# A decoder layer's start: the order of the first loads, who squares x, and where two projections stand

## The chip, the cores and the metric

The kernel runs on one core of one Trainium2 chip. The core has five engines that run side by side, each through its own list of instructions in order: PE (matrix products and transposes, into PSUM), DVE and POOL (elementwise work; POOL does not reach PSUM), ACT (elementwise functions, copies, scaling) and SP, which here only issues transfers (DMA). ACT can issue transfers too. The metric is the device time of one execution in microseconds; lower is better. One run of the kernel before was also profiled.

## The reference, cut to what matters

One layer, 512 tokens, width 1024, float32. It normalises x, makes one wide projection, and sends its columns through a state-space branch and an attention branch.

```python
h = rms_norm(x, norm_w[layer])
proj = h @ w_in[layer]
u_s, z_s, q, k, v, z_a, r_s, r_a = jnp.split(proj, offsets, axis=-1)
y_s = s5_branch(u_s, lam_re, lam_im, log_dt, b_re, b_im, c_re, c_im, d_skip, w_glu)
y_s = (y_s * jax.nn.silu(z_s)) @ w_ssm_out
q, k = rope(rms_norm(q, ...)), rope(rms_norm(k, ...))
y_a = (dilated_attention(q, k, v) * jax.nn.silu(z_a)) @ w_attn_out
m = jax.nn.sigmoid(r_s) * y_s + jax.nn.sigmoid(r_a) * y_a
x = x + m @ w_o
```

`s5_branch` is a linear recurrence over time with a complex diagonal A of 64 groups x 64 states, made from `lam_re`, `lam_im` and `log_dt`; B (`b_re`, `b_im`: 64 x 64 x 16 each) feeds it, C reads it. `dilated_attention` takes three groups of heads and joins them by their softmax sums.

## The kernel before, in words

**Precision and projections.** Each float32 operand of a large product is split into a rounded high part and a low rest, and `mm3` (L107) adds three products: high-high, high-low, low-high. A weight tile (128 rows x 8 x 128 columns, 512 KB) is loaded by `load_w` (L162) into `w_raw`, of which there are two buffers; ACT writes `w_hi` (L93), and DVE or POOL writes `w_lo` (L95); of these pairs there are three. `plan` (L112 to L149) lists all weight tiles in order, `get_w` takes the next one and calls for the loads two tiles ahead. A projection of 128 columns for all 512 tokens (`cm_unit`, L172) is 24 matmuls.

**The start.** SP loads x in four pieces of 512 KB (L193), with the first two weight tiles between them; for those two the low part is written by POOL (`lo_w`, L191). Tokens are taken in two halves. For each, ACT squares and sums two pieces (L208), DVE makes the reciprocal root in eleven small steps (L99, L210), ACT and DVE scale x (L214, L216), PE transposes it (L223), and ACT and DVE write the two parts of the transposed, normalised `hT` (L227, L228). The first three projections run on the first half of the tokens and then on the second (L287 to L292).

**The state-space tables.** `lam_re`, `lam_im` and `log_dt` are loaded by SP (L298 to L300), and some hundred small DVE operations make the powers of A from them (L303 to L378); PE transposes these into `AT` and `fT` (L388, L394). B is loaded into tile `dd` (L408): `D1` holds real over imaginary part, `D2` imaginary over real part, 64 partitions each, so each half of B is loaded twice (L411 to L414). POOL negates one half of `D2` (L415), and DVE and POOL make `BB` and `BB2` (L422 to L427).

**W and X units, scan, Y.** For each of eight blocks of groups, `w_unit` (L263) forms coefficients (`coef`, DVE and POOL) and transposes them to W on PE; `x_unit` (L275) reads the projection u back through DRAM (`ud`) and multiplies it by W into `Xs`. When all eight are there, the scan runs on DVE (`scan_work`, L636, lines 590 to 634). Then the Y loop (L770) makes outputs block by block and `g_unit` applies GELU.

**Fillers.** `order` (L127) lists projections that depend on `hT` alone: gates `za`, `zs`, `rs`, values `v0`, `v`, and the first `n_ra` of eight `ra` units. `filler()` takes the next one. They stand between W and X units (L656), beside the scan (ten, L761) and in the Y loop (one per block, the rest after). The remaining `ra` units stand around the last head pair's softmax (L1019, L1022): while DVE and ACT do the softmax, PE does `ra` units up to `KT - 2`, then `values`, then the last two. In the W and X part, W0 follows the sixth `u` projection, W1 and X0 the seventh, W2, X1, W3 and X2 the eighth (L442 to L444).

**Who sets the order.** The program is written in one stream. When it is built, a planner plays it through with modelled durations and gives each engine its list: whatever is ready by the model goes when the engine is free, and earlier lines go first. On the chip this order is fixed, and each instruction waits for its real inputs. A transfer that waits stands in its issuing engine's list, and what is behind it waits too.

Of the kernel before, what the change touches and what calls it, by code (L numbers as in the profile page):

```python
# [11 lines left out]
F32 = mybir.dt.float32  # L12
F32R = mybir.dt.float32r
I32 = mybir.dt.int32
AF = mybir.ActivationFunctionType
ALU = mybir.AluOpType
# [4 lines left out]
P = 128  # L21
D = 1024
S = 512
KT = D // P
NB = S // P
G = 64
# [26 lines left out]
def tile_hybrid_block(ctx: ExitStack, tc: tile.TileContext, x, positions, norm_w, w_in, lam_re, lam_im,  # L53
# [19 lines left out]
    def scr(shape, dtype=F32):  # L73
        n = int(np.prod(shape[1:]))
        o = scr_o[0]
        scr_o[0] += n
        assert scr_o[0] <= 4096
        v = scr_t[0:shape[0], o:o + n]
        if len(shape) == 3:
            v = v.rearrange("p (a b) -> p a b", b=shape[2])  # L80
        elif len(shape) == 4:
            v = v.rearrange("p (a b c) -> p a b c", b=shape[2], c=shape[3])
        return v if dtype == F32 else v.bitcast(dtype)
# [26 lines left out]
        pe.matmul(o, ll, rh, start=False, stop=last, skip_group_check=True)  # L110

    plan, loaded, look = [], [], 2  # L112
    n_ra = 2
    lo_w = [dve]

    def section(w, k0, k1, *cols):
# [35 lines left out]
    def prefetch(n):  # L152
        while len(loaded) < min(n, len(plan)):
            loaded.append(load_w(*plan[len(loaded)]))
# [5 lines left out]
        return loaded[i]  # L160

    def load_w(srcs, kts, cols):  # L162
        raw = wp.tile([P, kts, cols], F32, name="w_raw", tag="w_raw", bufs=2)
        w = cols // len(srcs)
        for i, s in enumerate(srcs):
            sp.dma_start(raw[:, :, i * w:(i + 1) * w], s.rearrange("(k p) c -> p k c", p=P))
        hi = wp.tile([P, kts, cols], F32R, name="w_hi", tag="w_hi")
        lo = wp.tile([P, kts, cols], F32R, name="w_lo", tag="w_lo")
        split(hi, lo, raw, lo_eng=lo_w[0])
        return hi, lo  # L170
# [14 lines left out]
    nps = bank("nps")  # L185
    pe.transpose(nps[:, 0:KT], nw8, ident[:KT, :KT])
    dve.tensor_copy(nwc, nps[:, 0:KT])
    x_all = big.tile([P, NB, D], F32, name="x_all", tag="s3")
    x_t = [x_all[:, r] for r in range(NB)]
    xv = x[0].rearrange("(i r) d -> r i d", r=NB)  # L190
    lo_w[0] = pool  # L191
    for r in range(NB):
        sp.dma_start(x_t[r], xv[r])  # L193
        if r in (1, 2):
            prefetch(len(loaded) + 1)
    lo_w[0] = dve
    hT_hi = cst.tile([P, KT, S], F32R, name="hT_hi")
    hT_lo = cst.tile([P, KT, S], F32R, name="hT_lo")

# [2 lines left out]
    rst = scr([P, NB])  # L202
    ra_ = scr([P, NB])
    rb_ = scr([P, NB])
    junk = big.tile([P, D], F32, name="junk", tag="s6a")
    for h in range(2):
        for r in (2 * h, 2 * h + 1):
            act.activation(junk, x_t[r], AF.Square, accum_out=ss[:, r:r + 1])  # L208
        w = slice(2 * h, 2 * h + 2)
        dve.tensor_scalar(ms[:, w], ss[:, w], 1.0 / D, EPS, op0=ALU.mult, op1=ALU.add)  # L210
        rsqrt(rst[:, w], ms[:, w], [P, 2], ra_[:, w], rb_[:, w])
        for r in (2 * h, 2 * h + 1):
            if r % 2:
                act.activation(x_t[r], x_t[r], AF.Copy, scale=rst[:, r:r + 1])  # L214
            else:
                dve.tensor_scalar(x_t[r], x_t[r], rst[:, r:r + 1], None, op0=ALU.mult)  # L216
        for q in range(KT // 2):
            ps = bank("hps")
            pv = ps.rearrange("p (k r i) -> p k r i", k=2, r=2)
            for r in range(2):  # L220
                for k in range(2):
                    kk = 2 * q + k
                    pe.transpose(pv[:, k, r], x_t[2 * h + r][:, kk * P:(kk + 1) * P], ident)  # L223
            for k in range(2):
                kk, t = 2 * q + k, slice(256 * h, 256 * h + 256)
                src, w = ps[:, 256 * k:256 * k + 256], nwc[:, kk:kk + 1]
                act.activation(hT_hi[:, kk, t], src, AF.Copy, scale=w)  # L227
                dve.scalar_tensor_tensor(hT_lo[:, kk, t], src, w, hT_hi[:, kk, t].bitcast(F32),  # L228
                                         op0=ALU.mult, op1=ALU.subtract)
# [62 lines left out]
                mm3(ps[:, t], hi[:, k], lo[:, k], hT_hi[:, k, t], hT_lo[:, k, t], k == 0, k == KT - 1)  # L292
    for j in range(3):
        u_unit(j, first[j][1])
    lr = scr([G, N])
    li = scr([G, N])
    dt = scr([G, 1])
    sp.dma_start(lr, lam_re[0])  # L298
    sp.dma_start(li, lam_im[0])
    sp.dma_start(dt, log_dt.rearrange("o g -> g o"))  # L300


    def exp_exact(dst, src, shape, pfx):  # L303
# [101 lines left out]
        pool.tensor_scalar(A4[sl, 0, 1], ATv[sl, 1, h, :, 0], -1.0, None, op0=ALU.mult)  # L405


    dd = big.tile([P, 4, G, Q], F32, name="dd", tag="s1")  # L408
    D1, D2, BB, BB2 = (dd[:, i] for i in range(4))
    bv = [b_re[0].rearrange("g n q -> n g q"), b_im[0].rearrange("g n q -> n g q")]  # L410
    sp.dma_start(D1[0:64], bv[0])  # L411
    sp.dma_start(D1[64:128], bv[1])
    sp.dma_start(D2[0:64], bv[1])
    sp.dma_start(D2[64:128], bv[0])  # L414
    pool.tensor_scalar(D2[0:64], D2[0:64], -1.0, None, op0=ALU.mult)  # L415
    nca = 8 * 9 * Q
    abt = big.tile([P, 4096], F32, name="ab", tag="s5")
# [17 lines left out]
    def wx(*js):  # L435
        for j in js:
            if j < 8:
                Ws[j] = w_unit(j)
            if j > 0:
                x_unit(j - 1, Ws.pop(j - 1))  # L440

    for j in range(3, 8):  # L442
        u_unit(j)
        wx(*((), (), (0,), (1,), (2, 3))[j - 3])  # L444


    sza = cst.tile([P, NP, S], F32, name="sza")
# [205 lines left out]
        else:  # L653
            {"za": za_unit, "zs": zs_unit, "rs": rs_unit, "ra": ra_unit}[kind](c)

    for js in ((4,), (5, 6), (7, 8)):  # L656
        filler()
        wx(*js)

# [435 lines left out]
```

## Time and profile before

| what | value |
|---|---|
| device time, median of 3 runs | 743.52 us (743.5 to 743.62) |
| profiled execution, its own time | 745.33 us |
| its span, first to last instruction | 743.5 us |
| mean granted TensorE clock | 0.983 |
| PE matmul busy | 702.2 us (94%) |
| DVE busy | 468.4 us (63%) |
| ACT busy | 336.7 us (45%) |
| POOL busy | 168.7 us (23%) |
| data moved | 85.51 MB, mean 115 GB/s |

A line of the page reads: source line, engine, operation, output <- inputs, shapes, count; busy time and mean duration of one; idle time before, and who ended it. In the timeline a row begins with its start in us from the span's start and its duration; brackets at its end hold the idle time of the engine before it and what ended that. A "wait" row reads: who waited <- for whom: us in total, times, longest. `PEld` is PE's loading of weights, `SPq` and `ACTq` are the lists in which transfers are issued, so their duration is that of issuing, not of the transfer. The granted clock is 1.00 at full speed.

### The profile page before, as it was taken

Reading aid. Unit: us, or ns where it says so; the run is one execution under the profiler, and the core shown is the slowest. Engines: PE = TensorE matmul, PEld = TensorE weight load, DVE = VectorE, ACT = ScalarE, POOL = GpSimd, SP = SyncE. Lnnn points to the kernel's source line nnn. Section 1 sums busy time; section 2 is a strip of 40 time slices with the busy share of each in tenths; the row PEclk is TensorE's granted clock in tenths of the full one; section 3 lists DMA queues with packets and bytes.
Section 4 is the critical chain, followed back from the end, with each engine's and each line's share of the span. In section 5 each row is a group of like instructions: output and inputs, shape, how many; then the busy total and the mean of one; then the engine's idle time right before and its main releaser. Section 6 shows DMA issues by size and latency. Waiting matters only on the chain.

```text
span 743.5 us, 13321 instructions
## 1 busy us (share of the span) xinstructions
PE 702.2 (94%) x5221; PEld 615.8 (83%) x5221; DVE 468.4 (63%) x958; ACT 336.7 (45%) x628; POOL 168.7 (23%) x304
## 2 busy tenths in 40 slices
PE   3699999999979688999999999999999999999998
PEld 2687788788857477888899999899999989778997
DVE  6768757989867454674336679667747654536631
ACT  6443544233388574433143475464446435433310
POOL 3345631110001001550001224142304311200000
PEclk9899999999999899999999999999999999999999
DMA  9754654674637765447324212213211321356321
GB/s 203 129 143 110 159 114 105 144 178 118 120 101 138 136 132 143 154 133 217 91 80 120 86 57 85 59 30 98 85 46 57 95 77 57 109 179 226 124 100 57
DMA packets 156014, 85.51 MB, mean 115 GB/s; under 512 B 40232, under 2 KB 148144, under 8 KB 155824
## 3 DMA queue, kind: packets, MB, share of 16 engines
q1 hardware_dynamic: 155936, 84.66, 44.1%
q8 instruction: 41, 0.67, 0.4%
q14 instruction: 21, 0.17, 0.1%
q10 hardware_dynamic: 16, 0.00, 0.0%
HBM read 73.18 MB, written 11.47 MB: 114 GB/s over the span
## 4 chain that ended last, share of the span: by engine, by line
PE 78%; DMA 8%; DVE 6%; SPq 3%; ACT 2%; issue 2%; POOL 0%; DVEq 0%; ACTq 0%
PE pj L110 21%; PE pj L109 21%; PE pj L108 21%; DMA w_raw<-in_w_in_dram 4%; PE ot L926 3%; PE ptp L940 2%; PE sps L870 2%; PE qtp L827 1%; DMA kd<-kt 1%; DVE w_lo L95 1%; PE xps L282 1%; DMA dd<-kd 1%; PE wps L271 1%; DMA gd<-th 1%; DVE scn L610 1%
## 5 line engine op out<-in xcount | busy, mean ns | idle before, releaser
L93 ACT ACTIVATE w_hi<-w_raw 128x1024 fp32r<-128x1024 f32 x100 | 105.9, 1060 | 200.6 <-PE pj L109 89.4
L95 DVE TENSOR_TENSOR w_lo<-w_raw,w_hi 128x1024 fp32r<-128x1024 f32 x98 | 124.2, 1268 | 64.1 <-ACT w_hi L93 62.9
L108 PE MATMUL pj<-hT_hi,w_hi 128*128 128x512 f32 (+1 forms) x344 | 135.0, 395 | 9.7 <-ACT w_hi L93 5.6
L109 PE MATMUL pj<-w_lo,hT_hi 128*128 128x256 f32 x512 | 144.0, 281 | 0.0
L110 PE MATMUL pj<-w_hi,hT_lo 128*128 128x256 f32 x512 | 143.9, 281 | 0.0
L108 PE MATMUL pj<-w_hi,hT_hi 128*128 128x256 f32 x512 | 143.8, 281 | 0.0
L109 PE MATMUL pj<-hT_lo,w_hi 128*128 128x512 f32 (+1 forms) x344 | 133.5, 389 | 0.4 <-DVE hT_lo L228 0.4
L110 PE MATMUL pj<-hT_hi,w_lo 128*128 128x512 f32 (+1 forms) x344 | 133.3, 388 | 0.1
L109 PEld LDWEIGHTS pj<-w_lo,hT_hi 128*128 128x128 f32 x512 | 96.2, 188 | 1.4 <-issue 0.7
L108 PEld LDWEIGHTS pj<-w_hi,hT_hi 128*128 128x128 f32 x512 | 96.0, 188 | 1.1 <-issue 0.9
L110 PEld LDWEIGHTS pj<-w_hi,hT_lo 128*128 128x128 f32 x512 | 96.0, 188 | 0.7
L108 PEld LDWEIGHTS pj<-hT_hi,w_hi 128*128 128x128 f32 x344 | 67.0, 196 | 23.1 <-ACT w_hi L93 5.8
L110 PEld LDWEIGHTS pj<-hT_hi,w_lo 128*128 128x128 f32 x344 | 66.5, 193 | 14.5 <-issue 0.8
L109 PEld LDWEIGHTS pj<-hT_lo,w_hi 128*128 128x128 f32 x344 | 66.8, 194 | 13.5 <-DVE hT_lo L228 0.8
L814 POOL TENSOR_TENSOR rt<-qraw,tC 128x256 f32<-128x256 f32 x12 | 16.5, 1371 | 127.0 <-DVE qraw L807 93.0
L109 PE MATMUL pj<-w_lo,mT_hi 128*128 128x256 f32 x128 | 36.2, 283 | 0.0
L110 PE MATMUL pj<-w_hi,mT_lo 128*128 128x256 f32 x128 | 36.2, 283 | 0.0
L108 PE MATMUL pj<-w_hi,mT_hi 128*128 128x256 f32 x128 | 36.2, 283 | 0.0
L849 ACT ACTIVATE Pt<-Pt,st 128x256 f32<-128x256 f32 (+1 forms) x64 | 31.0, 487 | 5.0 <-DVE st L847 4.8
L799 DVE TENSOR_REDUCE ssq<-qsq 128x8 f32<-128x512 f32 x24 | 16.4, 685 | 26.3 <-ACT qsq L798 26.2
L835 ACT ACTIVATE qkp<-qtp,wcol 128x512 fp32r<-128x512 f32 (+1 forms) x32 | 20.7, 685 | 20.7 <-PE qtp L827 15.6
L796 ACT COPY qraw<-pj 128x512 f32<-128x512 f32 x24 | 14.1, 586 | 35.0 <-PE pj L110 34.8
(272 smaller groups left out, 1368.5 us busy)
## 6 DMA issues: line engine op xcount, KB each, us to landing
w_raw<-in_w_in_dram SPq DMA_DIRECT2D x40, 512.0 KB
w_raw<-in_w_in_dram SPq DMA_DIRECT2D x64, 256.0 KB
dd<-kd SPq DMA_DIRECT2D x8, 512.0 KB
w_raw<-in_w_glu_dram SPq DMA_DIRECT2D x8, 512.0 KB
w_raw<-in_w_ssm_out_dram SPq DMA_DIRECT2D x8, 512.0 KB
w_raw<-in_w_o_dram SPq DMA_DIRECT2D x8, 512.0 KB
x_all<-in_x_dram SPq DMA_DIRECT2D x4, 512.0 KB
ud<-uT SPq DMA_DIRECT2D x8, 256.0 KB
```

The source lines that it names most:

```text
L93: act.activation(hi, src, AF.Copy, scale=scale)
L95: e.tensor_tensor(lo, src, hi.bitcast(F32), op=ALU.subtract)
L108: pe.matmul(o, lh, rh, start=first, stop=False, skip_group_check=True)
L109: pe.matmul(o, lh, rl, start=False, stop=False, skip_group_check=True)
L110: pe.matmul(o, ll, rh, start=False, stop=last, skip_group_check=True)
L799: dve.tensor_reduce(sq[:, 2 * b:2 * b + 2], s.rearrange("p (r h d) -> p r h d", r=2, h=4), AX.X, ALU.add)
L814: pool.tensor_tensor(t1, rh[:, :, :, 0:16], cv.broadcast_to([P, NB * 2, 2, 16]), op=ALU.mult)
L835: act.activation(hi, ps[sl], AF.Copy, scale=w)
L849: act.activation(o, o, AF.Exp, bias=nm, scale=-1.0, accum_out=st[:, kind, 1, h, b:b + 1])
L870: pe.matmul(pss[h][:, cols], QT[x_][po, 0, cb], KA[y_][po, ks], start=n == 0, stop=n == 2, skip_group_check=True)
L926: pe.matmul(o, v, pts[h][:, (2 * i + k) * P:(2 * i + k + 1) * P], start=first, stop=kind == 1 and b == NB - 1 and k == 1, skip_group_check ...
L940: pe.transpose(ps[:, (2 * i + k) * P:(2 * i + k + 1) * P], Pt[:, h, kind, 2 * bb + i, k * P:(k + 1) * P], ident)
```

## The change

- `ra` units among the fillers: four instead of two; the filler loop between W and X units has five steps instead of three, and before it only W0 is made, after the eighth `u` projection.
- One chain of transfers on SP, tied in this order of issue: the four pieces of x, four weight tiles into a tile of their own (`w_early`, in the place that `Xs` takes later), the real and the imaginary half of B into `D1`, and then two copies inside SBUF from `D1` to `D2`.
- `load_w` takes the first four weights from `w_early` and issues no transfer for them; their split is called for inside the loop over token halves. POOL no longer writes low parts of weights there; DVE does.
- The loads of `lam_re`, `lam_im` and `log_dt` are issued by ACT at the start.
- Of each pair of x pieces ACT squares one and DVE the other (`tensor_tensor_reduce`).

```diff
-    n_ra = 2
+    n_ra = 4
...
     def load_w(srcs, kts, cols):
-        raw = wp.tile([P, kts, cols], F32, name="w_raw", tag="w_raw", bufs=2)
-        w = cols // len(srcs)
-        for i, s in enumerate(srcs):
-            sp.dma_start(raw[:, :, i * w:(i + 1) * w], s.rearrange("(k p) c -> p k c", p=P))
+        if len(loaded) < len(early):
+            raw = early[len(loaded)]
+        else:
+            raw = wp.tile([P, kts, cols], F32, name="w_raw", tag="w_raw", bufs=2)
...
+    lr = scr([G, N])
+    li = scr([G, N])
+    dt = scr([G, 1])
+    act.dma_start(lr, lam_re[0])
+    act.dma_start(li, lam_im[0])
+    act.dma_start(dt, log_dt.rearrange("o g -> g o"))
...
-    lo_w[0] = pool
-    for r in range(NB):
-        sp.dma_start(x_t[r], xv[r])
-        if r in (1, 2):
-            prefetch(len(loaded) + 1)
-    lo_w[0] = dve
+    early_t = big.tile([P, 4, KT, P], F32, name="w_early", tag="s2")
+    early = [early_t[:, i] for i in range(4)]
+    dd = big.tile([P, 4, G, Q], F32, name="dd", tag="s1")
+    D1, D2, BB, BB2 = (dd[:, i] for i in range(4))
+    moves = [(x_t[r], xv[r]) for r in range(NB)]
+    moves += [(early[i], plan[i][0][0].rearrange("(k p) c -> p k c", p=P)) for i in range(4)]
+    moves += [(D1[0:64], b_re[0].rearrange("g n q -> n g q")), (D1[64:128], b_im[0].rearrange("g n q -> n g q"))]
+    moves += [(D2[64:128], D1[0:64]), (D2[0:64], D1[64:128])]
+    queued_sp = None
+    for o, i in moves:
+        if queued_sp is None:
+            queued_sp = sp.dma_start(o, i)
+        else:
+            with tc.issue_after(queued_sp.ins):
+                n = sp.dma_start(o, i)
+            queued_sp = n
...
-    junk = big.tile([P, D], F32, name="junk", tag="s6a")
+    junk = big.tile([P, 2, D], F32, name="junk", tag="s6b")
     for h in range(2):
-        for r in (2 * h, 2 * h + 1):
-            act.activation(junk, x_t[r], AF.Square, accum_out=ss[:, r:r + 1])
+        act.activation(junk[:, 0], x_t[2 * h], AF.Square, accum_out=ss[:, 2 * h:2 * h + 1])
+        dve.tensor_tensor_reduce(junk[:, 1], x_t[2 * h + 1], x_t[2 * h + 1], 1.0, 0.0, ALU.mult, ALU.add,
+                                 ss[:, 2 * h + 1:2 * h + 2])
...
+        prefetch(h + 1)
         for q in range(KT // 2):
...
-    sp.dma_start(D1[0:64], bv[0])
-    sp.dma_start(D1[64:128], bv[1])
-    sp.dma_start(D2[0:64], bv[1])
-    sp.dma_start(D2[64:128], bv[0])
...
     for j in range(3, 8):
         u_unit(j)
-        wx(*((), (), (0,), (1,), (2, 3))[j - 3])
+    wx(0)
...
-    for js in ((4,), (5, 6), (7, 8)):
+    for js in ((1,), (2, 3), (4,), (5, 6), (7, 8)):
         filler()
         wx(*js)
```

More of the change, by code (lines that the diff above doesn't have):

```diff
@@ L162, in load_w @@
     def load_w(srcs, kts, cols):
-        raw = wp.tile([P, kts, cols], F32, name="w_raw", tag="w_raw", bufs=2)
-        w = cols // len(srcs)
-        for i, s in enumerate(srcs):
-            sp.dma_start(raw[:, :, i * w:(i + 1) * w], s.rearrange("(k p) c -> p k c", p=P))
+        if len(loaded) < len(early):
+            raw = early[len(loaded)]
+        else:
+            raw = wp.tile([P, kts, cols], F32, name="w_raw", tag="w_raw", bufs=2)
+            w = cols // len(srcs)
+            for i, s in enumerate(srcs):
+                sp.dma_start(raw[:, :, i * w:(i + 1) * w], s.rearrange("(k p) c -> p k c", p=P))
         hi = wp.tile([P, kts, cols], F32R, name="w_hi", tag="w_hi")
@@ L294, in tile_hybrid_block @@
         u_unit(j, first[j][1])
[L295 to L300, printed above, removed]
     def exp_exact(dst, src, shape, pfx):
@@ L405, in tile_hybrid_block @@
         pool.tensor_scalar(A4[sl, 0, 1], ATv[sl, 1, h, :, 0], -1.0, None, op0=ALU.mult)
-    dd = big.tile([P, 4, G, Q], F32, name="dd", tag="s1")
-    D1, D2, BB, BB2 = (dd[:, i] for i in range(4))
-    bv = [b_re[0].rearrange("g n q -> n g q"), b_im[0].rearrange("g n q -> n g q")]
-    sp.dma_start(D1[0:64], bv[0])
-    sp.dma_start(D1[64:128], bv[1])
-    sp.dma_start(D2[0:64], bv[1])
-    sp.dma_start(D2[64:128], bv[0])
     pool.tensor_scalar(D2[0:64], D2[0:64], -1.0, None, op0=ALU.mult)
```

## The prediction

> **What bounds the kernel now.** I read first a table of the span cut into stretches at the events that matter (each row: from:to, length, busy time of PE, of its weight loads, of DVE, ACT and POOL with instruction counts, granted TensorE clock, DMA share, GB/s).
>
> ```profile
> 0.00:12.80 12.80, 0.24 (x1) 0.18 (x1) 6.69 (x24) 6.58 (x9) 3.81 (x13) 1.00 0.96 257
> 12.80:31.08 18.28, 12.34 (x81) 11.65 (x81) 12.43 (x74) 7.98 (x15) 6.62 (x8) 0.94 0.97 126
> 31.08:45.83 14.75, 14.63 (x133) 14.15 (x133) 13.70 (x45) 9.60 (x18) 8.20 (x29) 0.84 0.21 48
> 45.83:71.16 25.33, 24.56 (x137) 19.44 (x134) 18.27 (x25) 8.51 (x11) 13.07 (x12) 1.00 0.59 162
> 71.16:117.06 45.90, 43.72 (x429) 35.57 (x430) 29.90 (x31) 24.64 (x41) 20.16 (x13) 0.96 0.59 137
> 117.06:207.33 90.27, 88.17 (x472) 71.23 (x469) 80.39 (x112) 33.03 (x57) 12.38 (x16) 1.00 0.59 134
> 207.33:290.20 82.87, 68.75 (x787) 54.97 (x788) 46.95 (x67) 58.10 (x129) 6.32 (x18) 0.92 0.61 121
> ```
>
> PE is the bound nearly everywhere. Its idle time lies at the start (12.6 us before 12.80), in 12.80:31.08 (5.9), in 71.16:117.06 (2.2), in 117.06:207.33 (2.1) and in 207.33:290.20 (14.1). From 117 to 207 the scan keeps DVE at 80 of 90 us, with projections beside it on PE; from 207 on PE waits for chains that begin where the scan ends. PE's waits before 120 us say who is late in front:
>
> ```profile
> PE hps L223 <- DVE x_all L216: 9.5, 1, 9.5
> PE pj L108 <- ACT w_hi L93: 5.6, 1, 5.6
> PE wps L271 <- DVE ab L254: 2.8, 2, 2.1
> ```
>
> The timeline shows why the first is 9.5 us (start, duration, engine, line, operation; in brackets the idle time before it and what ended it):
>
> ```profile
> 4.95 1.06 ACT L208 ACTIVATE junk<-x_all 128x1024 f32<-128x1024 f32 x1 [2.31 <-DMA x_all<-in_x_dram]
> 6.36 1.06 ACT L208 ACTIVATE junk<-x_all 128x1024 f32<-128x1024 f32 x1 [0.27 <-DMA x_all<-in_x_dram]
> 7.54 0.17 DVE L210 TENSOR_SCALAR scr<-scr 128x2 f32<-128x2 f32 x1 [3.61 <-ACT junk L208]
> 9.61 2.34 POOL L95 TENSOR_TENSOR w_lo<-w_raw,w_hi 128x1024 fp32r<-128x1024 f32 x1 [7.48 <-ACT w_hi L93]
> 9.72 2.25 DVE L105 SCALAR_TENSOR_TENSOR scr<-scr 128x2 f32<-128x2 f32 x1
> 12.01 0.75 DVE L216 TENSOR_SCALAR x_all<-x_all,scr 128x1024 f32<-128x1024 f32 x1
> 12.81 3.67 PE L223 MATMUL hps<-ident,x_all 128*128 128x128 f32 x16 [9.54 <-DVE x_all L216]
> ```
>
> The reader is to see that a two-column DVE instruction took 2.25 us instead of some 0.17, just while POOL ran its 2.34 us split of the first weight. Then the second wait, the third weight:
>
> ```profile
> 24.57 0.38 SPq L166 DMA_DIRECT2D w_raw<-in_w_in_dram  x1
> 25.23 0.72 DVE L484 CAST scr<-scr 128x4 f32<-128x4 int32 x1 [2.70 <-DMA scr<-in_positions_dram]
> 29.97 1.06 ACT L93 ACTIVATE w_hi<-w_raw 128x1024 fp32r<-128x1024 f32 x1 [7.22 <-DMA w_raw<-in_w_in_dram]
> 31.08 0.58 PE L108 MATMUL pj<-hT_hi,w_hi 128*128 128x256 f32 x1 [5.57 <-ACT w_hi L93]
> 30.00:35.00 5.00, 3.81 (x16) 3.52 (x17) 3.94 (x12) 4.97 (x11) 2.65 (x6) 0.50 0.54 153
> ```
>
> Its transfer is issued only at 24.57, behind the B transfers; ACT stands 7.22 us in front of it with the second half of hT behind that split, and PE starts again at 31.08 with the clock at 0.50.
>
> **The change part by part. Start.** x0 and x1 arrive as before (4.95, 6.36). The square of x1 goes to DVE. No row has that operation at 1024 columns; a row below has the same one at 256 columns for 0.42, so four times that, 1.7, is the upper bound, and the 1.22 of a two-input DVE operation on 1024 the lower; I take 1.3, nearer the one of equal size. It ends at 7.7, where the statistics began at 7.54. The small operations then ran 2.18 (7.54 to 9.72); without the POOL split beside them the last takes 0.2 instead of 2.25, so the scaling starts at 10.1 instead of 12.01: **-1.9**. The three small loads moved to ACT cost three issues of about 0.6 (as SP's of such size); the 2.31 ACT idled before 4.95 hides them; uncovered they cost up to 1.8.
>
> **Third weight.** Before the first use of four weights there are now only 4 MB on the queue. How fast that goes is in the DMA windows:
>
> ```profile
> 5.00:10.00 5.00, 0.00 (x0) 0.00 (x0) 2.08 (x12) 3.47 (x6) 0.39 (x1) 1.00 1.08 334
> 15.00:20.00 5.00, 4.64 (x25) 4.19 (x25) 4.83 (x20) 3.52 (x10) 1.54 (x1) 1.00 1.07 101
> 20.00:25.00 5.00, 5.00 (x45) 5.00 (x45) 2.54 (x17) 1.15 (x1) 1.85 (x1) 1.00 0.84 62
> ```
>
> With x0 in at 4.95 and 3.7 MB left at 334 GB/s the fourth weight lands at about 16, the third at 14.5. With its split (1.06 and 1.2 us) it is ready by 17 to 18, when PE is still on the second: the 5.6 us wait goes (**-5.6**), and with it the slow clock behind it: 4.7 us at half speed, of which 2.0 is won (**-2.0**; the rest I leave to DVE's pace there). What is late next is hT's second half. DVE gets two squares (2.6) and two splits (2 x 1.25) more, ACT loses two squares; from 10 to 31 DVE then has some 5 us more work and 3 us fewer POOL collisions, and where it idled (2.7 at 25.23) it can fill. I charge **+1.0**, between 0 and 4.
>
> **B and the copies.** Two loads of 256 KB in 64-byte pieces remain of four; at 62 to 101 GB/s they take 2.6 to 4.2 us each and land at 21 to 25. The two copies inside SBUF read what they write, so SP waits in front of each. No row has such a copy: from below 0.8 us (256 KB at 334 GB/s), from above 4.2, as for 64-byte pieces; rows of 4 KB are like x's, so I take 1, plus 2 for landing. D2 is then whole at 25 to 29. BB is first computed from it at 53.59, so some 25 us of other work on every engine cover this: **0**. ```profile
> 9.50 4.80 SPq L412 DMA_DIRECT2D dd<-in_b_im_dram  x1
> 53.59 1.21 DVE L423 TENSOR_TENSOR dd<-dd,fT 128x1024 f32<-128x1024 f32 x1
> ```
>
> What stands behind SP's wait in the worst order are the fifth and sixth weights, positions and the norm weights. That the queue holds everything behind a waiting transfer is seen here too:
>
> ```profile
> SPq L166 <- DVE w_lo L95: 260.2, 61, 14.0
> ```
>
> The Trainium skill, DMA: Bandwidth & Descriptors, section Anatomy of one DMA, says that DMA engines do not wait on semaphores, the issuing sequencer does; by that rule these copies would stop SP until B has landed, and the 14.0 us of the row agree with it. Its section Why small descriptors are slow (HBM only) would put the copies, as an estimate, near 0.6 us each; the sum would be the same.
>
> **W and X two projections later.** One projection is 24 matmuls, here from 52.16 to 57.86:
>
> ```profile
> 52.16 0.50 PE L108 MATMUL pj<-hT_hi,w_hi 128*128 128x512 f32 x1
> 57.63 0.39 PE L110 MATMUL pj<-hT_hi,w_lo 128*128 128x512 f32 x1
> ```
>
> I take 5.6. So 11.2 us more of PE work stand before the last X, and 11.2 less in the tail. The scan can start when the last X is out:
>
> ```profile
> 64.33 1.22 DVE L252 TENSOR_TENSOR ab<-dd,AT 128x1024 f32<-128x1024 f32 x1
> 75.97 1.34 PE L271 MATMUL wps<-ident,ab 128*128 128x128 f32 x8 [2.07 <-DVE ab L254]
> 78.39 0.63 PE L108 MATMUL pj<-hT_hi,w_hi 128*128 128x512 f32 x1
> 115.00 2.13 PE L282 MATMUL xps<-Uj,W 128*64 128x64 f32 x64
> 119.27 1.22 DVE L610 TENSOR_TENSOR scn<-Xs,scn 128x1024 f32<-128x1024 f32 x1
> ```
>
> With 8.5 us won in front and 11.2 put in, it starts 2.7 later; PE's 2.8 us of waits for W0 and W1 and some 1.4 of slow clock behind them (0.63 for a matmul that takes 0.39) can go, for W comes later on PE's path than the coefficients. That is worth 0 to 4.2, and less if DVE is late with its tables (down to -3); I take **-1.0**. The Trainium skill, TensorE: Matmul & The Clock Gate, section Part 1, ties the half clock to an idle window of about 3.4 us. By that rule a rest of 2 us would cost only itself; the trace differs, for after 2.07 at 75.97 the clock did fall. The sum by the rule would be 1.4 us better if such a rest stays.
>
> **Tail.** In the last head pair ra units 2 to 5 cover the softmax; now only 4 and 5, with 6 and 7 free to move up.
>
> ```profile
> 635.41 0.42 DVE L847 CUSTOM_DVE_ANT_0 Pt<-sps,maskA 128x256 f32<-128x256 f32 x1 [2.27 <-PE sps L870]
> 644.15 0.62 DVE L903 TENSOR_SCALAR Pt<-Pt,sfb 128x256 f32<-128x256 f32 x2
> 651.75 1.69 PE L940 MATMUL ptp<-ident,Pt 128*128 128x128 f32 x14
> 668.74 1.29 POOL L95 TENSOR_TENSOR aT<-at,aT 128x512 fp32r<-128x512 f32 x1 [24.63 <-ACT aT L93]
> 671.90 0.39 PE L108 MATMUL pj<-aT,w_hi 128*128 128x512 f32 x1
> ```
>
> PE came to the transposes 7.0 us after the last Pt (651.75 - 644.77), and to the first product with aT 1.9 us after aT was whole (671.90 - 670.03). So 8.9 of the 11.2 us of cover taken out were spare, and some of the rest too, as ra units also fill the time between the pieces of values. I charge **+1.5**, from 0 to 6 if the remaining units cannot be spread so well.
>
> Sum: -1.9 - 5.6 - 2.0 + 1.0 - 1.0 + 1.5 = **-8.0**. The profiled execution took 745.33 (span 743.5 and 1.8 around it), so 737.3 by its own time; the median of the runs is 743.52, 1.8 below, hence **735.5**.
>
> **The rivals.** *Tables early.* lam, its partner and log_dt are there at 4 us instead of behind x, and DVE has 3.61 us idle before 7.54. If the chain to A comes out 5 us or more sooner, PE never waits for W and nothing is charged to hT: 3.2 more (the rest of the 4.2) and 1.0 are won, and the tail may cost 0: 735.5 - 5.7 = 729.8. Against it: DVE is the engine that gets more work.
>
> *DVE waits for positions.* In the trace it stood 2.70 there, while hT_lo had to wait for ACT anyway; if positions now land at 29 and hT_lo of the second half stands behind them, PE's second half starts 4 to 5 us later than I have it: 740.
>
> *Cover too thin.* The tail costs 6 instead of 1.5, or PE's 14.1 us of idle in 207:290 grows by as much with another order: 740.
>
> *The change does not do what it says.* The tie between the transfers sets the order of issue, not of the work; if ACT and DVE still reach the second half of hT at 31, nothing is won in front, the scan starts 11 us later, and the shorter tail pays just that: 743.5.
>
> *Slower, by SP's wait.* If pieces and copies go at 4.8 us each, the longest issue of a B transfer (9.50 to 14.30), then from 16 on B lands at 26 and the copies at 35, positions at 37. If hT_lo is behind them, the first three projections, which need some 10 us from there, end at about 48 instead of 44.6 (45.83 less 1.2 for A's transposes); +3.5, the tail's +1.5 and W's -1.0 make 747.5. It decides from positions at 34 on. For it: positions are behind the chain in the program. Against it: the planner may issue whatever is ready while the copies are not, and positions need nothing.
>
> **How the numbers follow.** Forecast 735.5 (732 to 738.5): 0.45. Tables early 729.8: 0.15. Positions 740: 0.15. Cover 740: 0.10. No effect 743.5: 0.06. Slower 747.5: 0.09. About 0.2% is what a measurement can tell here from no change. Faster 0.85, within it 0.06, slower 0.09. The range 727.5 to 742.5 leaves out the last two and a little below; the likeliest case alone has 732 to 738.5.
>
> **What would show it.** PE's first transposes at about 10.8; no wait for w_hi near 31, clock 1.0 in 30:40; the first three projections done near 36; POOL without w_lo; the last X near 118 to 120 and the scan behind it as long as before; two ra units fewer after 630 and no PE idle there over 1 us. DVE standing for positions, SP for the copies with weights behind them, or a scan that starts past 125 would make it wrong.

## The result, and the profile after

The changed kernel is slower. Its median is 753.15 us (751.36 to 754.38) beside 743.51 us (742.16 to 743.62) for the kernel before: the ratio is 1.0132, with a 95% interval of 1.0104 to 1.0160. The forecast was 735.5, with a range of 727.5 to 742.5. The profiled execution took 751.98 us with a span of 750.2, so the span grew by 6.7 where the forecast took 8.0 off.

PE has the same work in both kernels and is busy for 94% and 93% of the span. So the change is best read as PE's idle time, place by place. These are the windows of both kernels, cut at the same five events: end of the first three projections, PE at the end of its work beside the scan, first product with `uss` (the scanned states), last transpose of Y, end. Columns: from:to, length, busy time of PE (count), of its weight loads, of DVE, ACT and POOL, granted clock, DMA share, GB/s. First before:

```profile
0.00:44.66 44.66, 26.05 (x179) 24.88 (x181) 31.64 (x140) 23.00 (x39) 18.63 (x48) 0.92 0.72 139
44.66:205.23 160.57, 157.62 (x1068) 127.34 (x1068) 129.38 (x168) 65.35 (x104) 45.61 (x41) 0.99 0.59 139
205.23:207.33 2.10, 0.00 (x0) 0.00 (x0) 0.35 (x1) 2.00 (x6) 0.00 (x0) 1.00 0.46 137
207.33:290.11 82.78, 68.66 (x786) 54.93 (x787) 46.95 (x67) 58.01 (x129) 6.32 (x18) 0.92 0.61 121
290.11:743.50 453.39, 449.82 (x3191) 408.65 (x3190) 260.05 (x584) 188.33 (x354) 98.12 (x197) 1.00 0.34 103
```

Then after:

```profile
0.00:41.45 41.45, 24.56 (x179) 23.73 (x181) 31.49 (x145) 21.66 (x36) 12.26 (x39) 0.96 0.74 168
41.45:220.10 178.65, 169.92 (x1117) 137.13 (x1116) 132.31 (x167) 65.13 (x102) 46.70 (x49) 0.98 0.56 131
220.10:226.24 6.14, 0.01 (x2) 0.01 (x1) 4.52 (x6) 5.97 (x12) 0.00 (x0) 0.73 0.29 86
226.24:304.20 77.96, 63.36 (x772) 50.71 (x773) 44.80 (x66) 56.96 (x128) 8.40 (x18) 0.96 0.57 122
304.20:750.20 446.00, 442.40 (x3157) 402.22 (x3156) 259.83 (x583) 186.06 (x350) 96.69 (x197) 1.00 0.33 101
```

Length less PE's busy time gives the idle time. Front: 18.6 before, 16.9 after (the forecast had 8.5 less, with the slow clock). From there to the end of PE's work beside the scan: 2.9, then 8.7. At the scan's end: 2.1, then 6.1. Y: 14.1, then 14.6. The rest: 3.6 in both. Altogether 41.3 became 49.9; PE's busy time fell by 1.9, to 700.2.

PE's waits up to the first product with `uss`, after the change (without one of 2.9 for the norm weight at the start and one of 0.4):

```profile
PE hps L245 <- DVE scr L335: 11.9, 1, 11.9
PE yps L742 <- ACT uss L730: 6.1, 1, 6.1
PE vtp L577 <- ACT vt L572: 5.2, 1, 5.2
PE pj L109 <- DVE hT_lo L250: 2.1, 2, 1.3
PE pj L110 <- DVE w_lo L95: 1.8, 1, 1.8
PE xps L304 <- DMA Uj<-ud: 1.2, 1, 1.2
```

The waits for the third weight (5.6) and for W's coefficients (2.8) are gone, as predicted. The first wait is 2.4 longer, a new one of 2.1 for hT lies in the first three projections, and two of 1.8 and 1.2 lie between these and the scan. In the scan stands a new wait of 5.2, and the one at its end is 4.0 longer.

**The start.** Timeline, DVE and PE:

```profile
6.34 1.23 DVE L228 CUSTOM_DVE_ANT_0 junk<-x_all 128x1024 f32<-128x1024 f32 x1 [2.41 <-DMA x_all<-in_x_dram]
10.14 1.22 DVE L228 CUSTOM_DVE_ANT_0 junk<-x_all 128x1024 f32<-128x1024 f32 x1 [0.91 <-DMA x_all<-in_x_dram]
13.05 1.22 DVE L95 TENSOR_TENSOR w_lo<-w_early,w_hi 128x1024 fp32r<-128x1024 f32 x1 [0.34 <-ACT w_hi L93]
14.26 0.75 DVE L237 TENSOR_SCALAR x_all<-x_all,scr 128x1024 f32<-128x1024 f32 x1
15.06 3.45 PE L245 MATMUL hps<-ident,x_all 128*128 128x128 f32 x16 [11.93 <-DVE scr L335]
```

The square on DVE took 1.23, as estimated. But behind it DVE's list put, ahead of the scaling of the first half, the square of the last piece (with 0.91 of waiting for it), the small operations of the second half, those of the step sizes, and the first weight's low part with a wait of 0.34. The scaling started at 14.26 instead of 12.01, the transposes at 15.06 instead of 12.81.

**Positions.** SP's list, then DVE and PE:

```profile
13.49 4.64 SPq L215 DMA_DIRECT2D dd<-in_b_im_dram  x1
18.17 3.57 SPq L169 DMA_DIRECT2D w_raw<-in_w_in_dram  x2
21.79 1.11 SPq L491 DMA_DIRECT2D scr<-in_positions_dram  x1
28.18 1.18 SPq L215 DMA_DIRECT2D dd<-dd  x2
26.97 0.17 DVE L493 CAST scr<-scr 128x4 f32<-128x4 int32 x1 [3.91 <-DMA scr<-in_positions_dram]
29.45 0.39 PE L109 MATMUL pj<-hT_lo,w_hi 128*128 128x256 f32 x1 [0.75 <-DVE hT_lo L250]
31.65 0.46 PE L109 MATMUL pj<-hT_lo,w_hi 128*128 128x256 f32 x1 [1.31 <-DVE hT_lo L250]
41.17 0.28 PE L110 MATMUL pj<-hT_hi,w_lo 128*128 128x256 f32 x1
```

Positions, 2 KB, were issued at 21.79 behind B and two further weights, and DVE stood 3.91 for them with the low part of hT's second half behind. PE then waited 0.75 and 1.31, and went on at half clock:

```profile
32.00:34.00 2.00, 2.00 (x11) 2.00 (x11) 2.00 (x8) 1.81 (x3) 1.42 (x1) 0.50 0.00 0
```

The first three projections ended at 41.45; before it was 44.66, and the forecast put it near 36.

**W, X and the scan.** Timeline, several engines:

```profile
120.44 1.03 PE L293 MATMUL wps<-ident,ab 128*128 128x128 f32 x8
129.35 2.13 PE L304 MATMUL xps<-Uj,W 128*64 128x64 f32 x64
133.62 1.22 DVE L619 TENSOR_TENSOR scn<-Xs,scn 128x1024 f32<-128x1024 f32 x1
173.06 0.39 SPq L169 DMA_DIRECT2D w_raw<-in_w_in_dram  x1
178.76 1.06 ACT L93 ACTIVATE w_hi<-w_raw 128x1024 fp32r<-128x1024 f32 x1 [11.73 <-DMA w_raw<-in_w_in_dram]
179.85 1.23 DVE L95 TENSOR_TENSOR w_lo<-w_raw,w_hi 128x1024 fp32r<-128x1024 f32 x1 [5.98 <-ACT w_hi L93]
180.34 1.11 PE L577 MATMUL vtp<-ident,vt 128*128 128x128 f32 x4 [5.24 <-ACT vt L572]
224.12 0.69 DVE L621 TENSOR_TENSOR Xs<-Xs,scn 128x512 f32<-128x512 f32 x1
```

PE is done with the last W at 121.5, then does 7.9 us of other work before the last two X. The scan starts at 133.62, not at 119.27 (+14.3; the forecast was 2.7, less 1.0 of waits), and takes 91.2 us instead of 86.3. In it one late weight lets ACT stand for 11.73 and DVE, in the middle of the scan, for 5.98; PE stands for 5.24 until ACT has written `vt`, a tile of values that PE transposes.

Where this other work comes from is seen in the list of PE's instructions as the program has it, which holds no times. The counts are matmuls or transposes in a row, up to the last X; the traces show the same order, with each `xps` product as two records (so x64 above for the 32 here):

```
before:  xps 16, wps 8, xps 16, wps 8, pj 3, xps 32     (195 pj of 128x512 ahead of the last xps)
after:   xps 16, wps 8, xps 16, pj 3, wps 8, pj 34, xps 32     (274 ahead)
```

The change means to put two projections, 48 matmuls, ahead of the last X. The list has 79 more, 3.3 projections. Most of the fifth filler, which is written ahead of W7, X6 and X7, stands between W7 and these X: 34 matmuls at the 0.233 of one are the 7.9 us.

### The profile page after: what moved, and what is told of

It reads as the page before. It is cut to its first block, busy times and chain, and to the rows that moved or that the text cites. A ratio compares the mean times of both kernels' runs of the same rounds, so it can differ in the third digit from the quotient of the medians.

```text
span 750.2 us, 13330 instructions
## 1 busy us (share of the span) xinstructions
PE 700.2 (93%) x5221; PEld 613.8 (82%) x5221; DVE 473.0 (63%) x964; ACT 335.8 (45%) x624; POOL 164.1 (22%) x302
## 4 chain that ended last, share of the span: by engine, by line
PE 60%; DMA 1%; DVE 0%; DVEq 0%; issue 0%
PE pj L109 17%; PE pj L110 17%; PE pj L108 17%; PE ot L935 3%; PE ptp L949 2%; PE sps L879 2%; PE qtp L836 1%; DMA dd<-kd 1%; PE sps L109 1%; PE sps L110 1%; PE sps L108 1%; DMA kd<-kt 0%; PE yps L740 0%; PE yps L742 0%; PE vtp L577 0%; PE yT L750 0%
## 5 line engine op out<-in xcount | busy, mean ns | idle before, releaser
L93 ACT ACTIVATE w_hi<-w_raw 128x1024 fp32r<-128x1024 f32 x96 | 101.7, 1060 | 199.7 <-PE pj L109 95.0
L95 DVE TENSOR_TENSOR w_lo<-w_raw,w_hi 128x1024 fp32r<-128x1024 f32 x96 | 121.6, 1268 | 70.5 <-ACT w_hi L93 69.6
L108 PE MATMUL pj<-hT_hi,w_hi 128*128 128x512 f32 (+1 forms) x344 | 132.9, 388 | 3.4 <-ACT th L478 3.4
L110 PE MATMUL pj<-hT_hi,w_lo 128*128 128x512 f32 (+1 forms) x344 | 131.4, 383 | 1.8 <-DVE w_lo L95 1.8
L108 PEld LDWEIGHTS pj<-hT_hi,w_hi 128*128 128x128 f32 x344 | 65.1, 190 | 17.3 <-ACT th L478 4.7
L109 PEld LDWEIGHTS pj<-hT_lo,w_hi 128*128 128x128 f32 x344 | 65.4, 190 | 14.7 <-DVE hT_lo L250 2.5
L823 POOL TENSOR_TENSOR rt<-qraw,tC 128x256 f32<-128x256 f32 x12 | 16.5, 1375 | 127.0 <-DVE qraw L816 92.7
L805 ACT COPY qraw<-pj 128x512 f32<-128x512 f32 x24 | 14.1, 586 | 35.0 <-PE pj L110 34.8
```

The lines of the kernel that those rows point to most:

```text
L93: act.activation(hi, src, AF.Copy, scale=scale)
L95: e.tensor_tensor(lo, src, hi.bitcast(F32), op=ALU.subtract)
L108: pe.matmul(o, lh, rh, start=first, stop=False, skip_group_check=True)
L109: pe.matmul(o, lh, rl, start=False, stop=False, skip_group_check=True)
L823: pool.tensor_tensor(t1, rh[:, :, :, 0:16], cv.broadcast_to([P, NB * 2, 2, 16]), op=ALU.mult)
```

## Experiments

Idle time of PE in the five places, as above (length of the stretch less PE's busy time), with the start of the scan, the median time, and its ratio to the kernel before in the same comparison. The single runs of one kernel spread over 0.2% (e8) to 1.2% (e5), so the intervals say what is told apart. The columns show where PE rests, but they do not add up to the time: PE's busy time differs too, from 699.9 (e9) to 704.4 (e7), and so does the granted clock (one run of e11 took 735.67 us at a mean of 0.995, another 741.15 at 0.986). The idle times are those of one profiled run of each kernel.

| run | front | to PE's end beside the scan | scan's end | Y | rest | scan starts | median us | ratio, 95% interval |
|---|---|---|---|---|---|---|---|---|
| before | 18.6 | 2.9 | 2.1 | 14.1 | 3.6 | 119.3 | 743.51 | |
| after | 16.9 | 8.7 | 6.1 | 14.6 | 3.6 | 133.6 | 753.15 | 1.0132 (1.0104 to 1.0160) |
| e1_ra_wx | 18.4 | 5.4 | 6.0 | 9.7 | 3.6 | 133.2 | 749.14 | 1.0064 (1.0039 to 1.0090) |
| e2_front | 16.5 | 5.1 | 6.0 | 12.8 | 3.6 | 125.4 | 748.49 | 1.0048 (1.0030 to 1.0065) |
| e3_actsq | 17.6 | 6.8 | 6.0 | 12.3 | 3.6 | 131.0 | 749.81 | 1.0071 (1.0044 to 1.0098) |
| e4_pos | 21.7 | 5.2 | 6.5 | 10.3 | 3.6 | 133.4 | 749.37 | 1.0073 (1.0045 to 1.0101) |
| e5_after_sw | 17.0 | 3.6 | 1.9 | 15.9 | 3.6 | 126.9 | 743.45 | 0.9979 (0.9954 to 1.0005) |
| e6_front_sw | 16.7 | 6.4 | 5.1 | 13.0 | 3.6 | 117.6 | 749.67 | 1.0083 (1.0052 to 1.0114) |
| e7_posq | 18.9 | 5.9 | 6.2 | 13.2 | 3.5 | 132.5 | 752.17 | 1.0113 (1.0091 to 1.0135) |
| e8_b4 | 19.0 | 9.0 | 6.3 | 13.8 | 3.6 | 135.7 | 754.06 | 1.0135 (1.0119 to 1.0152) |
| e9_wx_sw | 18.2 | 0.3 | 1.7 | 16.2 | 3.6 | 125.6 | 741.71 | 0.9959 (0.9935 to 0.9983) |
| e10_asq_sw | 18.1 | 0.8 | 1.7 | 17.2 | 3.6 | 124.5 | 745.28 | 1.0022 (0.9998 to 1.0046) |
| e11_small_asq_sw | 13.7 | 0.2 | 1.6 | 14.6 | 3.6 | 121.2 | 738.49 | 0.9915 (0.9882 to 0.9949) |
| e12_front_mended | 14.7 | 3.8 | 5.0 | 14.3 | 3.6 | 114.3 | 745.31 | 0.9997 (0.9980 to 1.0014) |

**The two halves of the change, each alone.** e1: the kernel before with this edit only:

```diff
-    n_ra = 2
+    n_ra = 4
...
-        wx(*((), (), (0,), (1,), (2, 3))[j - 3])
+    wx(0)
...
-    for js in ((4,), (5, 6), (7, 8)):
+    for js in ((1,), (2, 3), (4,), (5, 6), (7, 8)):
```

> The kernel before, with only the four ra fillers and the W and X units two projections later; loads and squares as before. As predicted (two projections cost 11.2 before the scan, less some 1 to 4.2 us of waits for W, and give 9.7 back in the tail): scan start at 126 to 129 us, time 742 to 745. Theory that these 11.2 us are not all, because the order also moves about one more projection (5 to 6 us) ahead of the last X, as in the changed kernel: scan start at 130 to 133, time 746 to 750. If the whole loss of the change sits here: about 753.

e2: the changed kernel with this edit taken back.

> The changed kernel with two ra fillers and the W and X units where they stood: only the order of the loads, the copies and the squares are changed. By the changed kernel's trace the first three projections end at 41.2 instead of 44.7 us, so if that carries through: scan start at 116, time 740. As I had predicted it (8.5 us from the front): 735. If what is gained at 41 us is lost again because W's coefficients, and not PE, set the last X: scan start at 119 to 121, time 743 to 746. If the new order of loads itself costs later: over 747.

Both halves are slower by themselves, 0.64% and 0.48%, and the whole is about their sum. PE's waits in e1:

```profile
PE yps L733 <- ACT uss L721: 6.0, 1, 6.0
PE vtp L568 <- ACT vt L563: 5.3, 1, 5.3
```

They are the two new waits of the changed kernel, without any change in front: scan at 133.2, 274 matmuls ahead of the last X, and the time is that of the second theory, which counted one more projection. In e2:

```profile
PE yps L742 <- ACT uss L730: 6.0, 1, 6.0
PE wps L293 <- DVE ab L276: 3.6, 1, 3.6
```

There the first three projections end at 42.0, 2.6 sooner than before, and this buys nothing: PE comes to W0 3.6 ahead of its coefficients, the list has 220 matmuls ahead of the last X instead of 195, and at the scan's end PE waits 6.0. The prediction, taken for the front alone, gives 735; the time is that of the last case of the expectation, over 747.

**The start.** e3: squares on ACT again.

```diff
-        act.activation(junk[:, 0], x_t[2 * h], AF.Square, accum_out=ss[:, 2 * h:2 * h + 1])
-        dve.tensor_tensor_reduce(junk[:, 1], x_t[2 * h + 1], x_t[2 * h + 1], 1.0, 0.0, ALU.mult, ALU.add,
-                                 ss[:, 2 * h + 1:2 * h + 2])
+        for r in (2 * h, 2 * h + 1):
+            act.activation(junk[:, 0], x_t[r], AF.Square, accum_out=ss[:, r:r + 1])
```

> The changed kernel with both squares on ACT as before. Theory that DVE's square of the fourth piece and the first weight's low part, which stood ahead of the scaling, cost the start: transposes at 12.5 to 13 instead of 15.06, the first three projections 2 us sooner unless positions hold them (then no change), time 751 to 753. Rival, that PE's start does not reach the end since DVE waits for positions until 27 us all the same: 753, within 1 us.

The transposes start at 13.59 instead of 15.06, so the squares were 1.5 of the loss there. They do not start sooner still, since DVE's list has the statistics of the second half, which wait for the square of the last piece, ahead of the scaling of the first. The time is 749.81; its interval lies just below that of the changed kernel. That the first three projections still end at 41.6, since DVE waits 4.5 for positions, is what the first theory allowed; that the time falls all the same, by 3.3, was in neither, and e10 below does not repeat it.

**Positions.** e4 issues their load from ACT at the start; e7 puts it in SP's chain between the fourth weight and B (in both, the load is taken out where it stood):

```diff
+    pos_i = scr([P, NB], I32)
+    moves += [(pos_i, positions[0].rearrange("(i r) -> i r", r=NB))]
     moves += [(D1[0:64], b_re[0].rearrange("g n q -> n g q")), (D1[64:128], b_im[0].rearrange("g n q -> n g q"))]
```

> The changed kernel with the positions loaded by ACT at the start. Theory that DVE's wait for them (3.91 us, with hT's second half behind it) costs PE its 2.1 us of idle time and some 2 us at the low clock after it: no DVE wait over 1 us between 15 and 35, clock 1.0 in 30:40, first three projections done at 37 instead of 41.2, scan 2 to 4 us earlier, time 749 to 751. Rival, that the tables and W's coefficients set the scan's start: projections earlier, scan start unchanged, time 752 to 754. Rival, that the sines of the positions now stand ahead of the scaling: transposes at 16 or later.

> The changed kernel with the positions in the chain on SP, between the fourth weight and B; nothing else. Theory that DVE's 3.91 us wait for them costs PE 2.1 us and about 2 us at the low clock: no wait of DVE for positions, first three projections done at 37 to 38 instead of 41.2; if the order behind it is as before, PE then waits longer for W's inputs or the scan is 2 to 4 us sooner: time 749 to 751. Rival, that this is lost again at the scan's end (uss 6.1 grows by what was won in front): 752 to 754.

Neither did what the theory said. In e4 the last rival came true in front: the first steps of the sines, and the low parts of two more weights, now stood in DVE's list ahead of the scaling, so that the transposes start at 19.55 and the first three projections end at 45.6. Yet the time is 749.37: PE rests 3.5 less between there and the scan's start, and 4.3 less in Y. So 4 us at this point are not 4 us at the end. In e7 the stall was handed on, and the first three projections end at 44.3, later than the 41.45 of the changed kernel. DVE's waits between 15 and 32 us:

```profile
18.94 0.17 DVE L493 CAST scr<-scr 128x4 f32<-128x4 int32 x1 [1.09 <-DMA scr<-in_positions_dram]
28.39 0.26 DVE L529 TENSOR_SCALAR scr<-scr 128x192 f32<-128x192 f32 x1 [3.88 <-DMA scr<-in_q_norm_w_dram]
```

It stood 3.88 at the same place for the norm weights, the next load of the list, and the time, 752.17, cannot be told from that of the changed kernel.

**The copies of B.** e8 loads all four halves from DRAM, in the chain.

```diff
-    moves += [(D2[64:128], D1[0:64]), (D2[0:64], D1[64:128])]
+    moves += [(D2[64:128], b_re[0].rearrange("g n q -> n g q")), (D2[0:64], b_im[0].rearrange("g n q -> n g q"))]
```

> The changed kernel with all four halves of B loaded from DRAM, in the chain, without copies inside SBUF. As predicted the copies cost and win nothing at the end (0), but the two loads are 4.8 us each at most ahead of positions: DVE waits 5 to 10 us longer for positions, first three projections at 46 to 50, time 755 to 760. If B's pieces take only the 0.5 to 1 us of issue that they take behind each other: within 2 us of 753.

DVE waits 5.5 for positions instead of 3.91, and the first three projections end at 44.0 instead of 41.45; the time, 754.06, is the same within the intervals. So the copies cost nothing that is measured, as predicted, and save 2.5 us in front that do not arrive at the end.

**The order ahead of the last X.** e5 is the changed kernel, e6 the front alone (e2), e9 the late W and X alone (e1), each with the last W and X units written ahead of the last filler:

```diff
-    for js in ((1,), (2, 3), (4,), (5, 6), (7, 8)):
+    for js in ((1,), (2, 3), (4,), (5, 6)):
         filler()
         wx(*js)
+    wx(7, 8)
+    filler()
```

(in e6 with the steps that the kernel before has).

> The changed kernel with W7, X6 and X7 written ahead of the fifth filler instead of behind it: PE's list has 240 instead of 274 full matmuls of projections ahead of the last X (before the change: 195). Theory that the loss sits in PE running out of work before the scan's end, because the scan starts 14 us late with 3.3 more projections ahead of it: scan start 34 x 0.233 = 7.9 us sooner, at 125 to 127, PE's wait of 6.1 for uss at the scan's end gone or under 2.5, time 5 to 6 us less, 747 to 748.5. Rival, that the last X is held by W's coefficients or by the loads of u, not by PE's list: PE waits for X 3 us or more there, scan start at 130 or later, time 751 to 754.

> The kernel of the run with the front alone (748.49), with W7, X6 and X7 ahead of the last filler: 191 instead of 220 matmuls ahead of the last X. Same theory: scan start at 118 to 119.5 instead of 125.35, the 6.0 us wait for uss gone or under 2.5, time 742 to 744, so that the front alone is neither gain nor loss. Rival (last X held by its inputs): scan start 122 or later, time 746 to 749.

> The kernel before with four ra fillers and the W and X units two projections later (as in the run that took 749.14), and W7, X6 and X7 written ahead of the fifth filler: 240 instead of 274 matmuls ahead of the last X, loads and squares as before. Theory that the late placement costs only by what PE's list puts ahead of the last X: scan start at 125 to 126.5 instead of 133.2, the waits for vt (5.3) and uss (6.0) gone or under 2.5 each, time 740 to 744. Rival, that in the changed kernel it needed the front as well: 746 to 750.

e5 takes back the whole loss by an order alone: 743.45 instead of 753.15 in the medians, more than the 5 to 6 us that the theory gave (the profiled executions differ by 6.2 in span, and by 7.8 in PE's idle time; that of e5 was the slowest of its ten runs). The last X now follows three matmuls after the last W, so it was the list, and not its inputs, that had held it. PE's wait at the scan's end, in e5:

```profile
PE yps L744 <- ACT uss L732: 2.0, 1, 2.0
```

The wait for `vt` is gone. In e9, too, both waits are gone or short, and that kernel is faster than the kernel before. There PE is idle for 0.3 us between the first projections and the end of its work beside the scan, instead of 2.9. But e6 does not follow (749.67 where the theory gave 742 to 744), and with it falls the simple theory that the scan's start decides. Its scan starts at 117.6, as the theory had it and 7.7 sooner than in e2, and ends at 208.4, only 1.2 sooner:

```profile
157.73 0.69 DVE L621 TENSOR_TENSOR scn<-scn 128x512 f32<-128x512 f32 x1
165.29 1.22 DVE L95 TENSOR_TENSOR w_lo<-w_raw,w_hi 128x1024 fp32r<-128x1024 f32 x1 [6.87 <-ACT w_hi L93]
```

In DVE's list the steps of the scan stand between the low parts of the weights for the projections beside it, and one of these came late. A scan that starts sooner does not find these weights ready sooner. In the runs named here the scan took 84 to 86 us where DVE stood 4.9 to 7.0 for weights in it (before, e2, e5, e9, e11) and 90 to 92 where it stood 8.1 to 11.9 (e1, e6, e12, changed kernel). That these stands are what lengthens the scan is read from the traces; what delays those weights (which transfer ahead of them in the queue) was not tried, so the cause stays open there.

**Mending the front.** e10 is e5 with both squares on ACT; e11 has besides the positions and the two norm weights in the chain ahead of B (their loads are taken out where they stood):

```diff
+    pos_i = scr([P, NB], I32)
+    moves += [(pos_i, positions[0].rearrange("(i r) -> i r", r=NB))]
+    qkw = scr([P, 2, NG, HD])
+    moves += [(qkw[:, i].rearrange("p g d -> p (g d)"), w.rearrange("g d -> (g d)").unsqueeze(0).to_broadcast([P, NG * HD]))
+              for i, w in enumerate((q_norm_w[0], k_norm_w[0]))]
```

> The changed kernel with W7, X6 and X7 ahead of the fifth filler (743.45) and both squares on ACT. If the 3.3 us that the squares alone gave (753.15 to 749.81) add up: transposes at 13.5, the time 740 to 741.5. Rival, that PE's earlier start is taken up by DVE's wait for positions and by the scan's end: 743 to 745.

> As the run with both squares on ACT and W7, X6, X7 ahead of the fifth filler, with positions and the q and k norm weights in SP's chain between the fourth weight and B. Theory that DVE's stand between 22 and 27 us goes only when every small load it meets in turn is early (with positions alone, DVE stood 3.9 for the norm weight at the same place): DVE's waits there together under 1.5, PE's waits for hT under 1, first three projections at 37 to 39, time 1 to 3 below the run without it. Rival, that the norm weights, asked for ahead of hT's low part, now hold hT's first half: PE waits 2 us or more near 18, no gain.

e10 is no faster than e5, as its rival said (745.28, just over its 743 to 745): transposes at 13.83, but DVE still waits 4.4 for positions, and the first three projections end at 43.0. e11 is the fastest kernel of the study, 738.49, 0.85% under the kernel before, and wins more over e10 than the 1 to 3 us expected. Its first two stretches and the scan's end:

```profile
0.00:40.62 40.62, 26.95 (x181) 25.57 (x183) 30.36 (x147) 22.86 (x39) 13.96 (x38) 1.00 0.74 165
40.62:207.38 166.76, 166.59 (x1115) 134.85 (x1114) 130.06 (x164) 68.74 (x109) 46.72 (x50) 1.00 0.59 139
207.38:209.02 1.64, 0.00 (x1) 0.00 (x1) 0.41 (x1) 1.57 (x5) 0.00 (x0) 1.00 0.00 0
```

PE is idle for 0.2 in 167 us. The transposes start at 12.94 (12.81 before), no sooner than in the kernel before, and the first projections end at 40.6, later than the 37 to 39 expected, although DVE stands behind no transfer between 13 and 41 us. PE rests only 1.0 in these 27.7 us; a part of them is a slow PE. Two matmuls of the same shape:

```profile
24.67 0.41 PE L108 MATMUL pj<-hT_hi,w_hi 128*128 128x256 f32 x1
25.04 0.28 PE L110 MATMUL pj<-hT_hi,w_lo 128*128 128x256 f32 x1
```

Up to 24.67 they follow each other every 0.21 us, from 25.04 on every 0.12; in the kernel before the quick pace began at 19.01. The sixteen transposes at 12.94 took 3.68, the sixteen at 27.90 took 1.91. So the clock of 1.00 in the first row does not describe the time ahead of 25, and some 3 us (an estimate: 27 matmuls from 18.89 to 25.04 at twice the later spacing) of what this front could have won went there. Whether that is so in every run of e11, or was luck of this one, the one profile does not show.

e12 takes the late W and X away again from e11:

> The front alone in its mended form (both squares on ACT, positions and norm weights ahead of B), with two ra fillers and the W and X units where they stood before, the last three ahead of the last filler: 191 matmuls ahead of the last X, as before the change (195). Theory that PE, which is 4 us sooner through the first three projections, then meets W0 before its coefficients are made and the scan's end before DVE has done the scan, so that the front pays only together with the later W and X units: waits for W's coefficients of 3 to 6 us, for uss of 4 to 6, time 743 to 747. Rival, that the mended front pays by itself: waits for W under 2, time 738.5 to 741.

```profile
PE yps L740 <- ACT uss L728: 5.0, 1, 5.0
PE wps L296 <- DVE ab L279: 3.7, 1, 3.7
```

745.31, no difference from the kernel before, as the theory had it. The front by itself, even mended, pays nothing: PE gets to W0 and to the scan's end sooner and waits there for DVE. The late W and X by themselves, well ordered, win 0.41%; both together win 0.85%, with intervals that just overlap.

## Why the prediction was wrong

The span was to fall by 8.0 and grew by 6.7, 14.7 apart. Of that, 5.3 lie in front (8.5 forecast; the first three projections came 3.2 sooner, 41.45 against 44.66), and 9.4 behind it (0.5 forecast, 9.9 measured).

- **Start, -1.9: wrong, +2.25.** "The scaling starts at 10.1" counted the instructions that the scaling needs, not those that DVE's list has ahead of it. The square's own price (1.3, measured 1.23) was right, and the 2.25 us operation beside POOL's split is gone. What stands there now cost more than that: another piece's square, a second set of statistics, a weight's low part. With both squares on ACT (e3) 1.5 of it comes back.
- **Third weight, -5.6, and its slow clock, -2.0: the wait went, the slow clock came back.** No wait for a weight is left in the first three projections, and the third weight's low part is out at 17.84, where 17 to 18 was forecast, so the transfer times were right. But PE waits 2.1 for hT and runs at 0.50 for 3.4 us again. What is late next was named (hT's second half), and charged at +1.0; the charge was for DVE's pace, while the stall itself was positions (DVE stood 3.91), which the text held as a rival at 0.15. That rival had the wait right; its price of 740 had only the front in it.
- **B and the copies, 0: right** (e8). The slower rival priced B's issue well (4.64 for one) but not the queue behind it: positions were issued at 21.79, not at 37, since the copies were placed behind them. They stood behind the pieces and two weights instead. D2 was whole at 32.6, not at 25 to 29, but BB was first computed at 45.9, so the cover of 25 us was less and still enough.
- **W and X, "11.2 us more of PE work stand before the last X", less 1.0 of waits: this step failed most.** 2.8 of waits for W went, as it said. But the list holds 3.3 projections more, not 2, and the forecast took the scan "as long as before" whatever runs beside it. PE's rest of 5.2 in the scan and 4.0 more at its end are the price, and in e5, which changes nothing but that order, PE rests 0.1 in the scan and 1.9 at its end, and the time is that of the kernel before. The step also used the wrong measure. A scan that starts past 125 was to be the sign of failure; e9 starts it at 125.6 and is faster than before. With two more projections ahead of the scan a later start can be free; in these runs it was where PE did not rest in the scan and at its end.
- **Tail, +1.5: 0.** From the last transpose of Y on PE is idle for 3.5 to 3.6 us in every run. The cover taken out was indeed spare, and rival "cover too thin" is out: Y's rest is 14.6 instead of 14.1. (In the other runs it lies between 9.7 and 17.2; why was not tried.)
- **Tables early: true, and worth nothing here.** W0's first coefficients began at 55.28 instead of 64.33. PE, by its list, came to W0 at 74.80 all the same.
- **8.5 us in front as 8.5 us at the end: the premise under the sum.** e4 (4 us later in front, faster), e2 and e12 (2.6 and 3.6 sooner, no gain) show that it does not hold while W's coefficients and the scan wait for DVE. The rows of the kernel before spoke against it: PE already waited there for DVE, 2.8 for W's coefficients and 2.1 for the scan, and time won ahead of such a wait makes it longer unless DVE's work comes forward too. Nor was 8.5 reached in front: with both squares on ACT and no wait of DVE for a transfer after 13 us, e11 ends the first three projections 4.0 sooner than the kernel before.

## What to carry to other kernels

Where one engine is busy 94% of the time, add up its idle time by place before and after, and ask of each gain whether the next place can take it: time won ahead of a wait for another engine is only a longer wait, as in e2 and e12. When work is moved in a program whose order is fixed when it is built, count in the built list what stands ahead of the critical instruction; here one order had put 34 matmuls ahead of the last X, and the loss went when they were taken out. When a stall at a small load is removed, look at the next load in the same list, and move all of them: one alone won nothing that could be measured here (e7), and all of them are part of the fastest kernel (e11).

## What the runs showed of the hardware

- The granted clock fell to 0.50 after PE had been idle for 1.31 us, and 0.75 shortly before, in the changed kernel (31.65), and it stayed there for some 3.4 us. Windows ahead of the fall, within it, and behind it:

```profile
30.20:31.70 1.50, 0.19 (x2) 0.05 (x1) 1.50 (x8) 1.02 (x3) 0.17 (x1) 1.00 0.80 221
34.60:35.20 0.60, 0.60 (x5) 0.60 (x4) 0.60 (x5) 0.00 (x0) 0.60 (x1) 0.50 0.00 0
35.20:36.00 0.80, 0.80 (x9) 0.80 (x9) 0.73 (x6) 0.48 (x3) 0.36 (x2) 0.99 0.00 0
```

The Trainium skill, TensorE: Matmul & The Clock Gate, section Part 1, gives an idle window of about 3.4 us for the fall and a busy one of as long for the rise. The time at 0.50 here agrees with the rise; the fall came after much shorter rests, so in this kernel short waits that followed each other were not free.

- A load of 2 KB took from 21.79 to 26.97 to be of use, behind B and two weights in one queue. The Trainium skill, DMA: Bandwidth & Descriptors, section Queues, rings and completion order, says that each DMA engine takes what a queue holds in the order of its ring; the 5.2 us agree with that, and positions ahead of B and these weights (e7) were in use at 18.94.
- Two copies of 256 KB inside SBUF, issued from 28.18 to 29.36, were whole by 32.58, when POOL used them; of the two loads of as many bytes each in 64-byte pieces, with the weights ahead of them in the queue, one held SP for 1.70 and the other for 4.64.
